# Turning the encoder's memory tokens in 32x32 blocks on VectorE, with a DMA exchange, in place of TensorE transposes

## The chip, the core and the metric

The kernel runs on one core of one Trainium2 chip. The metric is the device time of one execution in microseconds (us); the median of three runs of the kernel before is 964.87 us (964.23 to 965.66).

The core has five engines with instruction queues of their own, and each queue runs in order: PE (TensorE, matrix products), DVE (VectorE), ACT (ScalarE), POOL (GpSimd) and SP (SyncE, which here issues nearly all DMAs). An engine waits for another by semaphores. So an instruction that waits holds up everything that stands behind it on its engine.

## What is computed

Two layers over 256 tokens of width 1024. Cut to what matters here:

```
mem_n = rms_norm(mem, mem_norm)                     # 256 memory tokens x 1024
for l in range(2):
    x = x + 0.5 * rms_norm(swiglu(rms_norm(x, ng[0]), w_gu[l, 0], w_down[l, 0]), ng[1])
    h = rms_norm(x, ng[2])
    tok, qm = retention_mixer(h, ...) if l == 0 else mla_mixer(h, ...)
    mem_out = memory_attention(qm, mem_n, mem_w_kv[l])   # keys and values: mem_n @ w_kv
    x = x + rms_norm(concat([tok, mem_out]) @ w_o[l], ng[3])
    x = x + 0.5 * rms_norm(swiglu(rms_norm(x, ng[4]), w_gu[l, 1], w_down[l, 1]), ng[5])
```

`swiglu(h) = (silu(g) * u) @ w_down` with `g, u = split(h @ w_gu)` and an inner width of 2816. The memory does not depend on x, so its norm and its transposed form, which the products with `mem_w_kv` need, can be made at any time before the mixer of the layer. The kernel makes them anew in each layer.

## The kernel before

**Precision and products.** Every float32 operand of a large product is split into a high part (fp32r, a copy made by ACT) and a rest (a subtraction on DVE); `split` (line 74) makes the two. A product is then three matmuls (`mm3`, lines 136 to 138): high x high, high x low of the weights, low x high. A weight tile arrives from HBM in a buffer `raw` (128x1024, five of them), ACT writes `wh`, DVE writes `wl` (nine of each), and PE uses both. `split_raw` does this for a tile. All loads are issued by SP in the order that the scheduler chose.

**The swiglu stage (`ffn`).** The inner width is cut into 11 chunks of 256 columns. For a chunk c, `gu(t, c)` makes the gate and up products of token half t (24 matmuls of 512 columns), `swiglu(t, c)` makes `s` on ACT and `a` on DVE, and the chunk's activations are turned for the product with `w_down`: `turn` lets DVE transpose 32x32 blocks into `aT`, and for a pair of chunks 4 POOL copies and 12 DMAs (32 KB each, issued by SP) exchange the blocks between the partitions into `ag` (one buffer). `take(c)` splits the result into `ah` and `al`; it stands behind the instructions of a later swiglu (`behind`, which queues instructions behind given ones on their engine). The program order from chunk 3 on is `gu(0, c)`, `gu(1, c)`, then the extra work of the chunk, then `both(c - 3)`, which is the down product of the chunk three before, 24 matmuls. PE follows this order exactly; ACT, DVE, POOL and SP follow an order that the scheduler computed when the program was built.

**The memory (`Mem`).** In the first swiglu of each layer extra work is hooked in at chunks 6, 7 and 8 (`mem_extra`): `load(mt)` loads the 128 memory tokens of half mt (two tiles `m`, 256 KB each) and the gain (512 KB, into a `raw` buffer), computes the norm (ACT squares, DVE `ms`, POOL `rstd`, DVE scales `m`); `put(mt)` lets PE transpose the eight 128x128 blocks into two banks, from where ACT and DVE split them into `zh` and `zl`. In layer 0 the extra work of chunks 3 and 4 makes the rotary tables: `posi`, `invb` and `lgb` are loaded, DVE computes `ang`, `kk`, `rr`, ACT the sine `tab`, DVE the rest of `tab`.

The names that the text uses: `raw`, `wh`, `wl` (weights), `s`, `a`, `aT`, `ag`, `ah`, `al` (activations of the swiglu), `m`, `ms`, `rstd` (memory and its norm), `zh`, `zl` (its transposed parts), `ang`, `kk`, `rr`, `tab` (rotary tables), `gpost`, `gpre`, `lgb`, `invb` (gains and small inputs).

Of the kernel before, what the change touches and what calls it, by code (L numbers as in the profile page):

```python
# [18 lines left out]
P = 128  # L19
DM = 1024  # L20
# [11 lines left out]
def kernel(ctx, tc, x, mem, positions, norm_gains, ffn_w_gu, ffn_w_down, w_o,  # L32
# [30 lines left out]
    def raw_tile():  # L63
        return wp.tile([P, 1024], F32, name="raw", tag="raw", bufs=5)
# [31 lines left out]
        return tc.issue_after(last_load[0])  # L96

    ahead = []

    def behind(*inss):  # L100

# [102 lines left out]
    def post(t, accs, gain, half, next_gain, hook=None):  # L204
# [19 lines left out]
                hook()  # L224
        return None if next_gain is None else pre(t, next_gain)


    def gu_src(wgu, c, u):
        return (wgu[2 * u * P:(2 * u + 2) * P, :]
# [2 lines left out]
    def ffn(l, j, zs, gains, extra=(), first=None):  # L232
        wgu, wd = ffn_w_gu[l, j], ffn_w_down[l, j]
        gu_w, d_w, act, at, pair = {}, {}, {}, {}, {}
        accs = [[None, None], [None, None]]
        extra = dict(extra)
        C = NFC - 1

        def load_gu(c):
            gu_w[c] = [weights(gu_src(wgu, c, u), 1024) for u in range(KB // 2)]  # L240

        def load_d(c):
            d_w[c] = [weights(wd[c * FC + b * P:c * FC + (b + 1) * P, :], 1024) for b in range(2)]

        def gu(t, c, part=None):
            z = zs[t]
            if c not in gu_w:
                load_gu(c)
            if part != 1:
                act[t, c] = bank()  # L250
            p = act[t, c]
            for k in range(KB) if part is None else range(part * 4, part * 4 + 4):
                wh, wl = gu_w[c][k // 2]
                n = slice((k % 2) * 512, (k % 2 + 1) * 512)
                m = slice(k * P, (k + 1) * P)
                mm3(p, z.h[:, m], z.l[:, m], wh[:, n], wl[:, n], k == 0, k == KB - 1)
            if part is None:
                swiglu(t, c)

        def swiglu(t, c):  # L260
            p, z = act[t, c], zs[t]
            s = k1("s")
            s_ins = S.activation(out=s, in_=p[:, 0:FC], func=AF.Silu, scale=z.r).ins  # L263
            a = k1("a")
            a_ins = V.scalar_tensor_tensor(out=a, in0=p[:, FC:2 * FC], scalar=z.r, in1=s,  # L265
                                           op0=ALU.mult, op1=ALU.mult).ins
            if (t, c) == (1, NFC - 1) or first and (t, c) == (0, 0):
                ahead[:] = [s_ins, a_ins]
            act[t, c] = a
            if c < C:  # L270
                turn(t, c)
            for k in [k for k in list(pair) if landed(k) == (t, c)]:
                with behind(s_ins, a_ins):
                    take(k)

        def turn(t, c):


            if t == 0 and c % 2 == 0:
                pair[c] = wk.tile([P, 1024], F32, name="aT", tag="aT", bufs=2)  # L280
            b = pair[c - c % 2]
            V.transpose(out=b.rearrange("p (q u t b x) -> p u t q b x", q=4, u=2, t=2, b=2)[:, c % 2, t],  # L282
                        in_=act.pop((t, c)).rearrange("p (b q x) -> p q b x", b=2, q=4))
            if t == 1 and c % 2:
                g = wk.tile([P, 1024], F32, name="ag", tag="ag", bufs=1)
                for i in range(4):
                    sl = slice(i * 32, (i + 1) * 32)
                    G.tensor_copy(out=g[sl, i * 256:(i + 1) * 256], in_=b[sl, i * 256:(i + 1) * 256])  # L288
                    for q in range(4):
                        if q != i:  # L290
                            nc.sync.dma_start(out=g[q * 32:(q + 1) * 32, i * 256:(i + 1) * 256],  # L291
                                              in_=b[sl, q * 256:(q + 1) * 256])
                pair[c - 1], pair[c] = g, g

        def landed(c):

            return (0, min(c + 3, C)) if c % 2 == 0 else (0, C) if c + 2 > C - 1 else (1, c + 2)

        def take(c):
            g = pair.pop(c)  # L300
            ah, al = t2("ah", 512, F32R), t2("al", 512, F32R)
            for t in range(2):
                sl = slice(t * FC, (t + 1) * FC)
                split(g.rearrange("p (i u t b x) -> p u t b i x", i=4, u=2, t=2, b=2)[:, c % 2, t],
                      ah[:, sl].rearrange("p (b i x) -> p b i x", i=4, b=2),
                      al[:, sl].rearrange("p (b i x) -> p b i x", i=4, b=2))
                at[t, c] = ah[:, sl], al[:, sl]

        def tr(t, c):
            a = act.pop((t, c))  # L310
            ah, al = k1("ah", FC, F32R), k1("al", FC, F32R)
            transposed([a[:, 0:P], a[:, P:2 * P]], ah, al)
            at[t, c] = ah, al

        def down(t, c, hs=(0, 1)):
            if c not in d_w:
                load_d(c)
            ah, al = at[t, c]
            for i in hs:
                if c == 0:  # L320
                    accs[t][i] = bank()
                for b in range(2):
                    wh, wl = d_w[c][b]
                    n = slice(i * 512, (i + 1) * 512)
                    m = slice(b * P, (b + 1) * P)
                    mm3(accs[t][i], ah[:, m], al[:, m], wh[:, n], wl[:, n],
                        c == 0 and b == 0, c == NFC - 1 and b == 1)

        def both(c):
            down(0, c)  # L330
            down(1, c)

        if first:
            gu_w[0] = first
            gu(0, 0, 0)
            zs[1].put()
            gu(0, 0, 1)
            swiglu(0, 0)
            gu(1, 0)
            gu(0, 1)  # L340
        else:
            gu(0, 0)
            gu(0, 1, 0)
            zs[1].put()
            gu(0, 1, 1)
            swiglu(0, 1)
            gu(1, 0)
        gu(1, 1)
        gu(0, 2)
        gu(1, 2)  # L350
        for c in range(3, C):
            gu(0, c)
            gu(1, c)
            if c == 4:
                with behind_weights():
                    gain_post, next_gain = gains()
            if c in extra:
                with behind_weights():
                    extra[c]()
            both(c - 3)  # L360
        gu(0, C)
        both(C - 3)
        tr(0, C)
        gu(1, C, 0)
        down(0, C - 2)
        down(0, C - 1)
        down(0, C)
        gu(1, C, 1)
        with in_order():
            z0 = post(0, accs[0], gain_post, True, next_gain, lambda: swiglu(1, C))  # L370
        down(1, C - 2)
        tr(1, C)
        down(1, C - 1)
        down(1, C, (0,))
        if z0:
            z0.put()
        down(1, C, (1,))
        z1 = post(1, accs[1], gain_post, True, next_gain)
        return [z0, z1]
# [36 lines left out]
    class Mem:  # L416
# [2 lines left out]
        def __init__(self, l):  # L419
            self.l = l  # L420

        def load(self, mt):
            if mt == 0:
                self.gain = raw_tile()
                bcast(self.gain, mem_norm)
                self.T = [ztile(), ztile()]
            parts = []
            for i in range(2):
                m_ = t2("m")
                nc.sync.dma_start(out=m_, in_=mem[0, mt * P:(mt + 1) * P, i * 512:(i + 1) * 512])  # L430
                parts.append(m_)
            r = rstd_of(parts, 1.0 / 32.0, EPS, "rstd")
            for i in range(2):
                V.scalar_tensor_tensor(out=parts[i], in0=parts[i], scalar=r, in1=halves(self.gain)[i],
                                       op0=ALU.mult, op1=ALU.mult)
            self.parts = parts

        def put(self, mt):
            for i in range(2):
                tp = transposes([self.parts[i][:, j * P:(j + 1) * P] for j in range(4)])  # L440
                sub = lambda a: a.rearrange("p (j m) -> p j m", j=4)[:, :, mt * P:(mt + 1) * P]
                split(tp.rearrange("p (j m) -> p j m", j=4), sub(self.T[i][0]), sub(self.T[i][1]))

        def keys(self):
            w = k_blocks(mem_w_kv[self.l], 0, 256)
# [642 lines left out]
        V.tensor_scalar(out=nlgb, in0=lgb[:, RH:2 * RH], scalar1=-1.0, scalar2=None, op0=ALU.mult)  # L1088

    def mem_extra(m):  # L1090
        def first():
            m.load(0)

        def second():
            m.put(0)
            m.load(1)

        def third():
            m.put(1)
        return {6: first, 7: second, 8: third}  # L1100

    m0 = Mem(0)
    zs = ffn(0, 0, zs, lambda: (gpost(0, 1), gpre(0, 2)), {3: tables, 4: tables2, **mem_extra(m0)}, first=first)
    zs = retention(zs, m0, lambda: (gpost(0, 3), gpre(0, 4)))
    zs = ffn(0, 1, zs, lambda: (gpost(0, 5), gpre(1, 0)))
    m1 = Mem(1)
# [37 lines left out]
```

## Time and profile before

| | |
|---|---|
| median of 3 runs | 964.87 us |
| the profiled execution | 965.5 us |
| its span (first to last instruction) | 963.7 us |
| PE busy | 949.9 us (99%) |
| DVE busy | 626.2 us (65%) |
| ACT busy | 516.2 us (54%) |
| POOL busy | 87.5 us (9%) |
| DMA queue of SP | 148608 packets, 188.38 MB, 61.2% |
| granted TensorE clock | 0.999 |

The profiled execution lies 1.8 us above its own span and 0.6 us above the median. A matmul's duration in the profile overlaps the next one's, since matmuls are pipelined; what a matmul costs is the distance between the starts of two that follow each other.

### The profile page before, as it was taken

How to read it: one execution, taken by the hardware profiler on the slowest of the kernel's cores; microseconds unless marked ns; L12 is line 12 of the kernel's file. 1: busy time of each engine (PE TensorE's matmuls, PEld its weight loads, DVE VectorE, ACT ScalarE, POOL GpSimd, SP SyncE). 2: the span in 40 equal slices, each digit the busy share in tenths (PEclk: the TensorE clock that was granted, in tenths of full speed). 3: DMA queues.
4: the chain of work that ended last, by engine and by line, in shares of the span. 5: the costliest groups of instructions: out<-in, count | busy, mean ns of one | idle time of the engine just before them, and what ended most of it. 6: DMA issues, size and time to landing. Idle time of an engine off the chain costs nothing.

```text
span 963.7 us, 13202 instructions
## 1 busy us (share of the span) xinstructions
PE 949.9 (99%) x4503; PEld 789.2 (82%) x4503; DVE 626.2 (65%) x989; ACT 516.2 (54%) x859; POOL 87.5 (9%) x122
## 2 busy tenths in 40 slices
PE   8999999999999999999999999999999999999997
PEld 6887888898878888888887888888897888888886
DVE  6766567586886775655558656655666886566552
ACT  6535456465665654544446444555568864444441
POOL 0110111010000111101101111101010011111010
PEclk9999999999999999999999999999999999999999
DMA  8668677493645556867546676875561746777631
GB/s 276 213 221 274 208 226 249 133 313 103 208 156 162 153 149 234 288 209 211 173 127 204 217 243 223 260 240 165 155 204 32 231 125 198 238 238 225 221 104 44
DMA packets 148679, 189.23 MB, mean 196 GB/s; under 512 B 13314, under 2 KB 130818, under 8 KB 148611
## 3 DMA queue, kind: packets, MB, share of 16 engines
q1 hardware_dynamic: 148608, 188.38, 61.2%
q8 instruction: 35, 0.57, 0.2%
q14 instruction: 34, 0.27, 0.1%
q10 hardware_dynamic: 2, 0.00, 0.0%
HBM read 179.42 MB, written 1.05 MB: 187 GB/s over the span
## 4 chain that ended last, share of the span: by engine, by line
PE 81%; DMA 7%; DVE 4%; ACT 3%; issue 3%; SPq 2%; POOL 0%; DVEq 0%; POOLq 0%; ACTq 0%
PE bank L138 26%; PE bank L136 26%; PE bank L137 26%; DMA raw<-in_ffn_w_gu_dram 4%; PE bank L162 2%; DVE wl L76 2%; ACT wh L75 2%; SPq L291 1%; DMA raw<-in_ret_w_in_dram 1%; DMA raw<-in_ffn_w_down_dram 1%; PE bank L493 1%; SPq L87 1%; ACT e L504 0%; DMA gpre<-in_norm_gains_dram 0%; DVE x L220 0%
## 5 line engine op out<-in xcount | busy, mean ns | idle before, releaser
L76 DVE TENSOR_TENSOR wl<-raw,wh 128x1024 fp32r<-128x1024 f32 (+2 forms) x326 | 388.6, 1209 | 164.6 <-ACT wh L75 158.2
L75 ACT CAST wh<-raw 128x1024 fp32r<-128x1024 f32 (+2 forms) x326 | 334.7, 1042 | 216.5 <-PE bank L138 78.4
L136 PE MATMUL bank<-wh,zh 128*128 128x512 f32 (+2 forms) x944 | 364.5, 386 | 0.6 <-ACT zh L75 0.4
L137 PE MATMUL bank<-wl,zh 128*128 128x512 f32 (+2 forms) x944 | 360.4, 382 | 0.6 <-DVE wl L76 0.6
L138 PE MATMUL bank<-wh,zl 128*128 128x512 f32 (+2 forms) x944 | 360.5, 382 | 0.4 <-DVE zl L76 0.4
L138 PEld LDWEIGHTS bank<-wh,zl 128*128 128x128 f32 x944 | 177.4, 188 | 35.4 <-DVE zl L76 1.4
L136 PEld LDWEIGHTS bank<-wh,zh 128*128 128x128 f32 x944 | 177.6, 188 | 34.8 <-ACT zh L75 0.9
L137 PEld LDWEIGHTS bank<-wl,zh 128*128 128x128 f32 x944 | 177.6, 188 | 34.5 <-DVE wl L76 1.6
L136 PE MATMUL bank<-wh,ah 128*128 128x512 f32 x352 | 138.0, 392 | 0.0
L138 PE MATMUL bank<-wh,al 128*128 128x512 f32 x352 | 137.4, 390 | 0.6 <-DVE al L76 0.6
L137 PE MATMUL bank<-wl,ah 128*128 128x512 f32 x352 | 137.0, 389 | 0.0
L288 POOL COPY ag<-aT 32x256 f32<-32x256 f32 x80 | 55.9, 699 | 481.6 <-DMA raw<-in_ffn_w_gu_dram 290.2
L263 ACT ACTIVATE s<-bank,rstd 128x256 f32<-128x256 f32 x88 | 41.5, 472 | 101.0 <-PE bank L138 100.9
L265 DVE SCALAR_TENSOR_TENSOR a<-bank,rstd,s 128x256 f32<-128x256 f32 x88 | 42.3, 480 | 59.5 <-ACT s L263 59.3
L138 PEld LDWEIGHTS bank<-wh,al 128*128 128x128 f32 x352 | 66.1, 188 | 15.2 <-DVE al L76 1.5
L137 PEld LDWEIGHTS bank<-wl,ah 128*128 128x128 f32 x352 | 66.1, 188 | 13.4
L136 PEld LDWEIGHTS bank<-wh,ah 128*128 128x128 f32 x352 | 66.1, 188 | 13.4 <-ACT ah L75 0.2
L147 ACT ACTIVATE junk<-bank 128x512 bf16<-128x512 f32 x24 | 14.3, 594 | 41.8 <-DVE y L209 29.4
L282 DVE STREAM_TRANSPOSE aT<-a 128x256 f32<-128x256 f32 x80 | 35.4, 443 | 1.5
L75 ACT CAST zh<-bank 128x512 fp32r<-128x512 f32 (+2 forms) x58 | 25.3, 462 | 19.4 <-PE bank L162 12.4
L76 DVE TENSOR_TENSOR zl<-bank,zh 128x512 fp32r<-128x512 f32 (+2 forms) x58 | 28.7, 519 | 6.0 <-ACT zh L75 6.0
L76 DVE TENSOR_TENSOR al<-ag,ah 128x256 fp32r<-128x256 f32 x80 | 31.3, 404 | 1.0 <-ACT ah L75 0.8
(154 smaller groups left out, 519.6 us busy)
## 6 DMA issues: line engine op xcount, KB each, us to landing
raw<-in_ffn_w_gu_dram SPq DMA_DIRECT2D x352, 256.0 KB, 4.7
raw<-in_ffn_w_down_dram SPq DMA_DIRECT2D x88, 512.0 KB, 5.4
raw<-in_ret_w_in_dram SPq DMA_DIRECT2D x48, 256.0 KB, 4.7
raw<-in_w_o_dram SPq DMA_DIRECT2D x16, 512.0 KB, 4.3
ag<-aT SPq DMA_DIRECT2D x240, 32.0 KB, 1.9
raw<-in_mem_w_kv_dram SPq DMA_DIRECT2D x8, 512.0 KB, 5.4
gpost<-in_norm_gains_dram SPq DMA_DIRECT2D x6, 512.0 KB, 6.2
gpre<-in_norm_gains_dram SPq DMA_DIRECT2D x5, 512.0 KB, 7.6
```

The lines of the kernel that those rows point to most:

```text
L75: ins = S.copy(out=hi, in_=src).ins
L76: V.tensor_tensor(out=lo, in0=src, in1=hi.bitcast(F32), op=ALU.subtract)
L87: last_load[0] = nc.sync.dma_start(out=dst[:, k], in_=src[:, k]).ins
L136: T.matmul(out=dst, lhsT=ah, rhs=bh, start=start, stop=False)
L137: T.matmul(out=dst, lhsT=ah, rhs=bl, start=False, stop=False)
L138: T.matmul(out=dst, lhsT=al, rhs=bh, start=False, stop=stop)
L147: S.activation(out=junk[:, :h.shape[1]], in_=h, func=AF.Square, scale=scale, accum_out=ss[:, i:i + 1])
L162: T.transpose(out=tp[:s.shape[1], j * P:(j + 1) * P], in_=s, identity=ident)
L263: s_ins = S.activation(out=s, in_=p[:, 0:FC], func=AF.Silu, scale=z.r).ins
L265: a_ins = V.scalar_tensor_tensor(out=a, in0=p[:, FC:2 * FC], scalar=z.r, in1=s, op0=ALU.mult, op1=ALU.mult).ins
L282: V.transpose(out=b.rearrange("p (q u t b x) -> p u t q b x", q=4, u=2, t=2, b=2)[:, c % 2, t], in_=act.pop((t, c)).rearrange("p (b q x) - ...
L288: G.tensor_copy(out=g[sl, i * 256:(i + 1) * 256], in_=b[sl, i * 256:(i + 1) * 256])
```

## The change

The four memory tiles and the gain are loaded together at chunk 3; the gain now lies in a buffer of the tag `A` (two buffers), not in a `raw`. The norms are made at chunks 4 and 5, each queued behind the swiglu just before (`latest`). At chunk 6 `turn(0)` lets DVE transpose one half of the columns of both token halves in 32x32 blocks into `mT`, and `exchange` (which is the code that stood in the swiglu's `turn`) makes 4 POOL copies and 12 DMAs into `mg`. At chunk 8 `take(0)` splits it and `turn(1)` does the other half of the columns; chunk 9 takes that. PE's 32 transposes of the memory are gone. The rotary tables keep their chunks 3 and 4, after the memory's part of the same chunk.

```diff
+    def exchange(b, g):
+        for i in range(4):
+            sl = slice(i * 32, (i + 1) * 32)
+            G.tensor_copy(out=g[sl, i * 256:(i + 1) * 256], in_=b[sl, i * 256:(i + 1) * 256])
+            for q in range(4):
+                if q != i:
+                    nc.sync.dma_start(out=g[q * 32:(q + 1) * 32, i * 256:(i + 1) * 256],
+                                      in_=b[sl, q * 256:(q + 1) * 256])
...
+            latest[:] = [s_ins, a_ins]
...
-        def load(self, mt):
-            if mt == 0:
-                self.gain = raw_tile()
...
-        def put(self, mt):
-            for i in range(2):
-                tp = transposes([self.parts[i][:, j * P:(j + 1) * P] for j in range(4)])
...
+        def load(self):
+            self.gain = wk.tile([P, DM], F32, name="mgain", tag="A", bufs=2)
+            bcast(self.gain, mem_norm)
+            self.T = [ztile(), ztile()]
+            self.parts = [[t2("m") for i in range(2)] for mt in range(2)]
+            for mt in range(2):
+                for i in range(2):
+                    nc.sync.dma_start(out=self.parts[mt][i], in_=mem[0, mt * P:(mt + 1) * P, i * 512:(i + 1) * 512])
+        def norm(self, mt):
+            parts = self.parts[mt]
+            with behind(*latest):
+                r = rstd_of(parts, 1.0 / 32.0, EPS, "rstd")
...
+        def turn(self, i):
+            b = wk.tile([P, 1024], F32, name="mT", tag="A", bufs=2)
+            with behind(*latest):
+                for mt in range(2):
+                    V.transpose(out=b.rearrange("p (q u j x) -> p u q j x", q=4, u=2, j=4)[:, mt],
+                                in_=self.parts[mt][i].rearrange("p (j q x) -> p q j x", j=4, q=4))
+            self.g = wk.tile([P, 1024], F32, name="mg", tag="A", bufs=2)
+            exchange(b, self.g)
...
+        def take(self, i):
+            th, tl = self.T[i]
+            with behind(*latest):
+                for mt in range(2):
...
+                    split(self.g.rearrange("p (i u j x) -> p u j i x", i=4, u=2, j=4)[:, mt], sub(th), sub(tl))
...
-        return {6: first, 7: second, 8: third}
+        def eighth():
+            m.take(0)
+            m.turn(1)
+        return {3: m.load, 4: lambda: m.norm(0), 5: lambda: m.norm(1), 6: lambda: m.turn(0), 8: eighth,
+                9: lambda: m.take(1)}
```

The order that the scheduler made of it changes in more places than these. First SP in the first swiglu of layer 0, from the gate and up loads of chunks 0 to 3 to those of chunk 6 (two rows of 256 KB make one `raw` tile; the 12 rows `ag<-aT` are one exchange). Before:

```order
L87 DMA raw<-in_ffn_w_gu_dram 128x2x256 x2
L291 DMA ag<-aT 32x256 x12
L87 DMA raw<-in_ffn_w_gu_dram 128x2x256 x6
L67 DMA gpost<-in_norm_gains_dram 128x1024
L67 DMA gpre<-in_norm_gains_dram 128x1024
L67 DMA lgb<-in_ret_log_decay_dram 128x12
L89 DMA raw<-in_ffn_w_down_dram 128x1024 x2
L87 DMA raw<-in_ffn_w_gu_dram 128x2x256 x3
L597 DMA invb<-in_inv_freq_dram 128x80
L87 DMA raw<-in_ffn_w_gu_dram 128x2x256 x2
L291 DMA ag<-aT 32x256 x12
L87 DMA raw<-in_ffn_w_gu_dram 128x2x256 x3
```

And now, on the same engine from the same exchange:

```order
L235 DMA ag<-aT 32x256 x12
L87 DMA raw<-in_ffn_w_gu_dram 128x2x256 x8
L67 DMA gpost<-in_norm_gains_dram 128x1024
L67 DMA gpre<-in_norm_gains_dram 128x1024
L67 DMA lgb<-in_ret_log_decay_dram 128x12
L89 DMA raw<-in_ffn_w_down_dram 128x1024 x2
L87 DMA raw<-in_ffn_w_gu_dram 128x2x256
L435 DMA m<-in_mem_dram 128x512 x2
L235 DMA ag<-aT 32x256 x12
L435 DMA m<-in_mem_dram 128x512 x2
L614 DMA invb<-in_inv_freq_dram 128x80
L87 DMA raw<-in_ffn_w_gu_dram 128x2x256 x7
```

Chunk 4's first tile moved behind the first exchange; of chunk 5's eight half tiles one stands before the second exchange and seven behind it, two memory tiles and `invb`, where five stood before it and three behind.

Next DVE in the same stage, from the second half of chunk 4's work to the first `al` of chunk 2. Before:

```order
L76 TENSOR_TENSOR wl<-raw,wh 128x1024 x3
L265 SCALAR_TENSOR_TENSOR a<-bank,rstd,s 128x256
L282 STREAM_TRANSPOSE aT<-a 128x4x64
L76 TENSOR_TENSOR wl<-raw,wh 128x1024 x4
L265 SCALAR_TENSOR_TENSOR a<-bank,rstd,s 128x256
L76 TENSOR_TENSOR al<-ag,ah 128x256
```

And now, from the last `kk` through chunk 5's four weight tiles into the `rr` that stand ahead of that `al`:

```order
L627 TENSOR_SCALAR kk<-kk 128x320
L76 TENSOR_TENSOR wl<-raw,wh 128x1024 x2
L276 SCALAR_TENSOR_TENSOR a<-bank,rstd,s 128x256
L294 STREAM_TRANSPOSE aT<-a 128x4x64
L76 TENSOR_TENSOR wl<-raw,wh 128x1024
L152 SCALAR_TENSOR_TENSOR ms<-ss 128x1
L442 SCALAR_TENSOR_TENSOR m<-m,rstd,mgain 128x512 x2
L76 TENSOR_TENSOR wl<-raw,wh 128x1024
L630 SCALAR_TENSOR_TENSOR rr<-kk,ang 128x160 x2
L76 TENSOR_TENSOR wl<-raw,wh 128x1024
L632 SCALAR_TENSOR_TENSOR rr<-kk,rr 128x320
```

The first part of the tables (`ang`, `kk`) now stands ahead of all four `wl` of chunk 5, the norm of the first memory half ahead of the fourth of them, and the rest of the tables (`rr`, `tab`) between there and the `al`; before, all of it stood ahead of the rows shown.

Last DVE in the first swiglu of layer 1, from the fourth `wl` of chunk 5 to the first `al` of chunk 2. Before:

```order
L76 TENSOR_TENSOR wl<-raw,wh 128x1024 x3
L265 SCALAR_TENSOR_TENSOR a<-bank,rstd,s 128x256
L76 TENSOR_TENSOR al<-ag,ah 128x256
L282 STREAM_TRANSPOSE aT<-a 128x4x64
L76 TENSOR_TENSOR al<-ag,ah 128x256
```

And now:

```order
L76 TENSOR_TENSOR wl<-raw,wh 128x1024
L276 SCALAR_TENSOR_TENSOR a<-bank,rstd,s 128x256
L294 STREAM_TRANSPOSE aT<-a 128x4x64
L76 TENSOR_TENSOR wl<-raw,wh 128x1024
L152 SCALAR_TENSOR_TENSOR ms<-ss 128x1
L442 SCALAR_TENSOR_TENSOR m<-m,rstd,mgain 128x512 x2
L76 TENSOR_TENSOR wl<-raw,wh 128x1024 x4
L276 SCALAR_TENSOR_TENSOR a<-bank,rstd,s 128x256
L76 TENSOR_TENSOR al<-ag,ah 128x256
L294 STREAM_TRANSPOSE aT<-a 128x4x64
L76 TENSOR_TENSOR al<-ag,ah 128x256
```

The norm of the first memory half moved from behind this `al` to a place ahead of it, with four `wl` in between.

## Rows read from the trace of the kernel before

**Rows 1.** The page: PE, its granted clock by slices, two groups of DVE.

```profile
PE 949.9 (99%) x4503; PEld 789.2 (82%) x4503; DVE 626.2 (65%) x989; ACT 516.2 (54%) x859; POOL 87.5 (9%) x122
...
PEclk9999999999999999999999999999999999999999
...
L265 DVE SCALAR_TENSOR_TENSOR a<-bank,rstd,s 128x256 f32<-128x256 f32 x88 | 42.3, 480 | 59.5 <-ACT s L263 59.3
...
L282 DVE STREAM_TRANSPOSE aT<-a 128x256 f32<-128x256 f32 x80 | 35.4, 443 | 1.5
```

**Rows 2.** Timeline of PE: start, us, engine, line, operation, tiles, shape, count [idle before].

```profile
121.95 0.40 PE L138 MATMUL bank<-wh,zl 128*128 128x512 f32 x1
122.18 1.04 PE L162 MATMUL bank<-ident,m 128*128 128x128 f32 x8
122.98 0.47 PE L136 MATMUL bank<-wh,ah 128*128 128x512 f32 x1
123.29 0.40 PE L137 MATMUL bank<-wl,ah 128*128 128x512 f32 x1
```

**Rows 3.** The memory's tile `m`, all its transposes: count, ns min/median/max.

```profile
L162 PE MATMUL bank<-ident,m x32: 270/272/276, 122.2 to 638.3; 128*128 128x128 f32 x32
```

**Rows 4.** Timeline of PE, first swiglu of layer 0: three matmuls.

```profile
56.26 0.50 PE L138 MATMUL bank<-wh,al 128*128 128x512 f32 x1
...
77.93 0.39 PE L137 MATMUL bank<-wl,zh 128*128 128x512 f32 x1
...
89.83 0.50 PE L138 MATMUL bank<-wh,al 128*128 128x512 f32 x1 [0.60 <-DVE al L76]
```

**Rows 5.** Timeline of DVE, 54 to 60 us.

```profile
54.25 1.22 DVE L76 TENSOR_TENSOR wl<-raw,wh 128x1024 fp32r<-128x1024 f32 x1 [1.97 <-ACT wh L75]
...
55.79 0.41 DVE L76 TENSOR_TENSOR al<-ag,ah 128x256 fp32r<-128x256 f32 x1
...
59.37 0.17 DVE L1088 TENSOR_SCALAR nlgb<-lgb 128x6 f32<-128x6 f32 x1 [1.37 <-DMA lgb<-in_ret_log_decay_dram]
```

**Rows 6.** Timeline of SP's queue, 45 to 73 us: loads, exchange, loads.

```profile
46.08 4.22 SPq L87 DMA_DIRECT2D raw<-in_ffn_w_gu_dram  x6
...
64.32 7.55 SPq L291 DMA_DIRECT2D ag<-aT  x12
71.92 1.26 SPq L87 DMA_DIRECT2D raw<-in_ffn_w_gu_dram  x2
```

**Rows 7.** Line 87's loads after an exchange: the two at 71.9 us, third and fourth at 47.5.

```profile
DMA to landing us min/median/max: 3.3/3.3/3.3
...
DMA to landing us min/median/max: 5.0/5.0/5.0
```

**Rows 8.** Timeline of DVE, 65 to 73 us: ends of the two parts of the rotary tables.

```profile
65.31 0.57 DVE L604 TENSOR_SCALAR ang<-invb,posf 128x80 f32<-128x80 f32 x2
...
68.20 0.33 DVE L610 TENSOR_SCALAR kk<-kk 128x320 f32<-128x320 f32 x1
...
69.58 0.55 DVE L613 SCALAR_TENSOR_TENSOR rr<-kk,ang 128x160 f32<-128x160 f32 x2
...
72.84 0.17 DVE L629 TENSOR_SCALAR tab<-tab 128x16 f32<-128x16 f32 x1
```

**Rows 9.** Timeline of DVE, 84 to 104 us: weights, the `al` of chunk 2, a norm.

```profile
84.35 4.71 DVE L76 TENSOR_TENSOR wl<-raw,wh 128x1024 fp32r<-128x1024 f32 x4
...
89.36 0.41 DVE L76 TENSOR_TENSOR al<-ag,ah 128x256 fp32r<-128x256 f32 x1
...
103.43 1.42 DVE L434 SCALAR_TENSOR_TENSOR m<-m,rstd,raw 128x512 f32<-128x512 f32 x2 [0.73 <-POOL rstd L141]
```

**Rows 10.** Timelines of SP, PE and DVE, first swiglu of layer 1.

```profile
561.31 8.42 SPq L291 DMA_DIRECT2D ag<-aT  x12
...
588.09 0.39 PE L138 MATMUL bank<-wh,al 128*128 128x512 f32 x1
...
583.30 0.42 DVE L76 TENSOR_TENSOR al<-ag,ah 128x256 fp32r<-128x256 f32 x1
```

More of the change, by code (lines that the diff above doesn't have):

```diff
@@ L98 @@
     ahead = []
+    latest = []
     def behind(*inss):
@@ L285, in turn @@
                 g = wk.tile([P, 1024], F32, name="ag", tag="ag", bufs=1)
[L286 to L292, printed above, removed]
+                exchange(b, g)
                 pair[c - 1], pair[c] = g, g
@@ L420, in __init__ @@
             self.l = l
-        def load(self, mt):
-            if mt == 0:
-                self.gain = raw_tile()
-                bcast(self.gain, mem_norm)
-                self.T = [ztile(), ztile()]
-            parts = []
-            for i in range(2):
[L429 to L436, printed above, removed]
@@ L438, in put @@
-        def put(self, mt):
-            for i in range(2):
-                tp = transposes([self.parts[i][:, j * P:(j + 1) * P] for j in range(4)])
-                sub = lambda a: a.rearrange("p (j m) -> p j m", j=4)[:, :, mt * P:(mt + 1) * P]
-                split(tp.rearrange("p (j m) -> p j m", j=4), sub(self.T[i][0]), sub(self.T[i][1]))
+        def load(self):
[6 more added lines that the diff above has]
+                    nc.sync.dma_start(out=self.parts[mt][i], in_=mem[0, mt * P:(mt + 1) * P, i * 512:(i + 1) * 512])
@@ new lines, in norm @@
+        def norm(self, mt):
+            parts = self.parts[mt]
+            with behind(*latest):
+                r = rstd_of(parts, 1.0 / 32.0, EPS, "rstd")
+                for i in range(2):
+                    V.scalar_tensor_tensor(out=parts[i], in0=parts[i], scalar=r, in1=halves(self.gain)[i],
+                                           op0=ALU.mult, op1=ALU.mult)
+        def turn(self, i):
[6 more added lines that the diff above has]
+            exchange(b, self.g)
@@ L444, in keys @@
+        def take(self, i):
+            th, tl = self.T[i]
+            with behind(*latest):
+                for mt in range(2):
+                    sub = lambda a: a.rearrange("p (j u i x) -> p u j i x", j=4, u=2, i=4)[:, mt]
+                    split(self.g.rearrange("p (i u j x) -> p u j i x", i=4, u=2, j=4)[:, mt], sub(th), sub(tl))
         def keys(self):
@@ L1090, in mem_extra @@
     def mem_extra(m):
[L1091 to L1099, printed above, removed]
-        return {6: first, 7: second, 8: third}
+        def eighth():
[3 more added lines that the diff above has]
+                9: lambda: m.take(1)}
     m0 = Mem(0)
-    zs = ffn(0, 0, zs, lambda: (gpost(0, 1), gpre(0, 2)), {3: tables, 4: tables2, **mem_extra(m0)}, first=first)
+    e0 = mem_extra(m0)
+    zs = ffn(0, 0, zs, lambda: (gpost(0, 1), gpre(0, 2)), {**e0, 3: lambda: (e0[3](), tables()), 4: lambda: (e0[4](), tables2())}, first=first)
     zs = retention(zs, m0, lambda: (gpost(0, 3), gpre(0, 4)))
```

## The prediction

> **What bounds the kernel now.** I read the page first: PE is busy 99% of the span, in every slice at a granted clock of nine tenths or more, which is the upper of its two levels (2.4 GHz) [rows 1]. DVE has a third of its time free and ACT nearly half. So a matmul that goes is worth its distance to the next, and nothing else in the kernel is worth anything unless PE waits for it. The timeline of PE says what that distance is: a matmul of 512 columns starts 0.23 us after the one before (121.95 to 122.18) [rows 2]. Then I looked for the places where PE comes close to waiting, because the change moves work on the queues behind it. In the first swiglu of layer 0 there are two, both at the third matmul of a down product, the first that needs `al`. At 56.26 PE starts as soon as the `al` of DVE at 55.79 has ended (55.79 + 0.41 = 56.20) [rows 4, 5]. At 89.83 it has waited 0.60 for the `al` at 89.36 [rows 4, 9]. There DVE has no slack at all: the `al` stands in its queue behind `wl` of weights, these behind `wh` of ACT, these behind loads, and the loads behind an exchange on SP. In layer 1 the same `al` ends at 583.72 and is used at 588.09: 4.4 us of slack [rows 10].
>
> **What goes.** The 32 transposes run in four groups of eight. Eight start at 122.18, the next matmul at 122.98, and the one after 0.31 later instead of 0.23 [rows 2]: 0.80 + 0.08 = 0.88 us per group, 3.5 us in all. All four groups lie behind the places treated below, so the gain is not eaten by them.
>
> The Trainium skill ("TensorE: Matmul & The Clock Gate", Part 4: PE-mode transpose) gives about 275 ns for a transpose in a kernel, and the trace has the same duration, 270 to 276 ns [rows 3]. But durations overlap: by starts one costs 0.11 us here. By the skill's figure the saving would be 32 x 0.275 = 8.8 us, an estimate from that page; by the starts it is 3.5, and the sum goes by these.
>
> **What comes, and is hidden.** Four DVE transposes of 512 columns per layer: 443 ns for 256 columns [rows 1], so between 0.44 and 0.89 each; I take 0.89, 3.5 us a layer, in chunks 6 and 8. Four exchanges of 12 issues, 7.6 to 8.4 us of SP each [rows 6, 10], with 16 POOL copies. The splits of the memory read `mg` instead of a bank, with the same count; I take no difference. By chunk 6 PE is late already (below), which gives the weights as much more slack; a swiglu chunk lasts 16 us of PE (72 matmuls), an exchange blocks SP for half of that, and its result is not needed before the mixer. The cost is nothing if it holds; if that cover were gone, the block of an exchange, 7.6 us, less the slack of the loads behind it (which I put at 4 at the least) would be 3 to 4 us per place. The gain tile no longer occupies a `raw`: worth nothing where PE does not wait for loads.
>
> **What is moved to where PE has no slack.** Three steps in layer 0.
>
> First, chunk 4's first tile now stands behind the first exchange, so DVE and ACT handle the third tile after it, not the second, ahead of the first `al`. Six loads took SP 4.22 us [rows 6], so two more make 1.4 us. DVE's `wl` at 54.25 [rows 5], which waits for the load, becomes one at 55.7, `al` ends at 57.6 and PE starts at 57.7 instead of 56.26: **1.4 us late**. Bounds: 0.6 (one load) and 2.0.
>
> Second, chunk 5. The `nlgb` that stands ahead of the next `al` waits for `lgb`, at 59.37 [rows 5]; two loads more ahead of it make 60.8. Then `a`, `al`, `aT`, `al`, about 1.5 us by their durations less overlaps, free the one `ag` buffer at 62.3 and SP starts the exchange, two us earlier than the 64.32 of before. It ends 7.55 us later [rows 6], at 69.9. Now come two memory tiles, 0.6 us each, and `invb`, issued at 71.1. The first two loads after an exchange land after 3.3 us, the third and fourth after 5.0 [rows 7]; `invb` is the third and lands at 76.1. DVE's `ang` and `kk` wait for it: 65.31 to 68.53 with one `wl` of 1.18 inside is 2.0 us [rows 8, 9], so 78.1. Two `wl` of 1.18 (4.71 for four [rows 9]): 80.5. `a` and `aT`, 0.48 + 0.44 [rows 1]: 81.4. Third `wl`: 82.6. The norm, the wait for `rstd` 0.73 and the scaling 1.42 [rows 9], with `ms` and the gaps between them about 2.3: 84.9. Fourth `wl`: 86.1. PE used its first `wl` of this chunk at 77.93 [rows 4], the fourth 18 matmuls later, at 82.0. So PE is **4.1 us late**, the 1.4 included. The loads of the last two tiles, issued up to 75.5, land by 81 and are not late themselves.
>
> Third, the `al` of chunk 2. Behind that `wl` DVE has the rest of the tables (69.58 to 73.01, the wait for ACT's `tab` included: 3.4 us [rows 8]), four `wl` (4.7), `a` and `aT` (0.9) and the `al` (0.41): 9.4 us, so it ends at 95.5, and PE's matmul of 89.83 starts then: **5.7 us late in all**. This includes the 0.6 that PE already waited there. Bounds for the three together: 3.7, if the loads behind the exchange land 2 us earlier (3.3 and not 5.0), and 7.7, if the wait for a slot or a lane adds as much as the 1 us by which layer 1's exchange exceeds this one, twice.
>
> Layer 1 has no tables. Its first exchange also has one tile more behind it, 1.3 us, so the second begins at about 562.6 where it began at 561.31 [rows 10], and takes 8 us: 570.6. Three memory tiles and then chunk 5's last tile are queued there; its second half is issued at 573.0 and lands 5.0 later, 578.0. `wh` and `wl`: 580.2. Then `a`, `aT` 0.9, `wl` 1.2, norm 2.3, four `wl` 4.7, `a` and `al` 0.9: 590.2. PE wants it at 588.09 [rows 10]: **2.0 us late**, between 0 and 3.5.
>
> **Sum.** 5.7 + 2.0 - 3.5 = +4.2 us. The profiled execution took 965.5 (span 963.7 and 1.8 around it); by it the new time is 969.7, and against the median of 964.87 it is **969.1**. Lower bound 3.7 + 0 - 3.5 = +0.2, upper 7.7 + 3.5 - 3.5 = +7.7.
>
> **Rivals.** *The waits fit in.* If loads behind an exchange land after 3.3 us throughout and DVE works while it waits now, layer 0 loses 3.7, layer 1 nothing: 965.1, no change. For it: the first two loads do land so, and DVE is idle a third of the time. Against: in before the third and fourth do not [rows 7], and DVE's queue is in order, so its idle time ahead of `ang` can't be used.
>
> *The gain stands alone.* PE loses only the first 1.4 us or nothing: 962.8 to 961.4. It needs chunk 5's first tile and `invb` to be there 4 us earlier, that is, a second exchange that starts at 58 and not 62. For it: nothing but the slack of 7 to 10 us that these tiles have in other chunks; against: the order puts seven of eight halves behind it.
>
> *A transpose costs PE its duration.* Then 8.7 us go (32 x 272 ns [rows 3]), and with the same waits 964.87 + 7.7 - 8.7 = 963.9. Against: the starts in [rows 2].
>
> *The exchanges delay weights too.* SP is held a further 7.6 us in chunks 6 and 8 of each layer. If the `al` of chunk 4 or the weights of chunk 9 come late by 3 us at one place in each layer, 975. It decides when a wait in SP's queue lasts beyond the 4 us of slack that I put above. Against it: PE's own lateness.
>
> **Chances.** Forecast 0.52, exchanges that delay weights too 0.10, waits fit in 0.17, gain alone 0.17, transposes at their duration 0.04. A change under 0.2% (1.9 us) can't be told from none. So slower 0.62, the same 0.17, faster 0.21. The forecast's own range is 966.8 to 972.6; with the rivals until two in ten are left out, 962.0 to 973.5.
>
> **What would show it.** PE's busy time down by some us, no `ident,m` rows; PE's waits in the first 100 us up from about 2 to about 7: at the third matmul of the first down product (57.7), at the last two weight tiles of chunk 5 (around 84), at the `al` of chunk 2 (95), and in layer 1 at the same `al`. SP's exchange at 62.3 and `invb` landing at 76. From 100 us on PE runs without waits to the mixer; the `mg` exchanges wait for nobody on PE. I am wrong if `invb` lands before 73, or if the `al` of layer 1 is there by 588, or if PE waits in chunks 7 to 10.

## The result and the profile after

The changed kernel takes 970.48 us (median of 12 runs, 966.3 to 973.98), the kernel before beside it 964.71: a ratio of 1.0062 (95% interval 1.0049 to 1.0074), slower by 5.8 us. The forecast was 969.1 and slower. The runs now scatter over 7.7 us, those of before over 3.9 (963.44 to 967.29, 12 runs).

The profiled execution took 972.66 us, its span is 970.9, so it lies 2.2 above the median and 7.2 above the span of before. From the page of the changed kernel, PE and its granted clock by slices, to be set beside [rows 1]:

```profile
PE 950.1 (98%) x4471; PEld 786.2 (81%) x4471; DVE 632.1 (65%) x997; ACT 515.5 (53%) x859; POOL 111.0 (11%) x138
...
PEclk9999999999999999999999999999999999999999
```

PE has 32 instructions fewer, as many as there were transposes, and is busy for as long as before. That can't be read as "the transposes were free": a stretch at a lower clock (below) makes busy time longer, and in the one kernel of the experiments that has none of the new waits (POOL, tables in `e`, norms at chunks 5 and 6) PE is busy 946.2 us, 3.7 less than before. The waits are in the span, not here. So the next view is what PE waited for, first in the kernel before, then in the changed one (us in total, times, longest):

```profile
PE bank L525 <- ACT pT L516: 1.4, 2, 0.9
...
PE bank L138 <- DVE al L76: 0.6, 1, 0.6
PE bank L137 <- DVE wl L76: 0.6, 2, 0.3
```

```profile
PE bank L139 <- DVE al L76: 4.0, 4, 2.0
PE bank L137 <- ACT ah L75: 2.7, 3, 1.5
...
PE bank L138 <- DVE wl L76: 2.2, 3, 1.7
...
PE bank L542 <- ACT pT L533: 0.4, 1, 0.4
```

`al`, `ah` and `wl` together made 1.2 us of waiting (PE's product lines moved by one) and now make 8.9. The timeline of PE says where (start, us, ..., [idle before]); each row is compared with the same matmul of before:

```profile
57.09 0.50 PE L137 MATMUL bank<-wh,ah 128*128 128x512 f32 x1 [1.51 <-ACT ah L75]
...
58.41 0.50 PE L139 MATMUL bank<-wh,al 128*128 128x512 f32 x1 [0.58 <-DVE al L76]
...
86.41 0.50 PE L138 MATMUL bank<-wl,zh 128*128 128x512 f32 x1 [1.69 <-DVE wl L76]
...
94.56 0.50 PE L139 MATMUL bank<-wh,al 128*128 128x512 f32 x1 [0.82 <-DVE al L76]
...
126.92 0.39 PE L137 MATMUL bank<-wh,ah 128*128 128x512 f32 x1
...
180.14 0.50 PE L137 MATMUL bank<-wh,ah 128*128 128x512 f32 x1 [0.68 <-ACT ah L75]
...
558.42 0.39 PE L138 MATMUL bank<-wl,ah 128*128 128x512 f32 x1
559.36 0.50 PE L139 MATMUL bank<-wh,al 128*128 128x512 f32 x1 [0.55 <-DVE al L76]
...
592.54 0.50 PE L137 MATMUL bank<-wh,ah 128*128 128x512 f32 x1 [0.55 <-ACT ah L75]
...
595.29 0.50 PE L139 MATMUL bank<-wh,al 128*128 128x512 f32 x1 [2.01 <-DVE al L76]
```

And three rows of PE in the kernel before that these are held against:

```profile
175.90 0.39 PE L136 MATMUL bank<-wh,ah 128*128 128x512 f32 x1
...
555.22 0.39 PE L137 MATMUL bank<-wl,ah 128*128 128x512 f32 x1
555.45 0.39 PE L138 MATMUL bank<-wh,al 128*128 128x512 f32 x1
```

Read as lateness: 58.41 - 56.26 [rows 4] = 2.15; at 86.41 it is 4.4, the fourth weight tile having been used at 82.0 before; 94.56 - 89.83 [rows 4] = 4.73; 126.92 - 122.98 [rows 2] = 3.94, one group of transposes less; 180.14 - 175.90 = 4.24 after two groups, so 1.2 was lost between; 558.42 - 555.22 = 3.20 at the start of layer 1 (the mixer gave back 1.0: the wait for `pT` shrank); 559.36 - 555.45 = 3.91; 595.29 - 588.09 [rows 10] = 7.20. All of this is one execution, and not the median one. Behind the last wait comes the last surprise, which windows show (stretch, length, busy us of PE, PEld, DVE, ACT, POOL, granted clock, DMA share, GB/s):

```profile
590.00:596.00 6.00, 3.44 (x14) 2.23 (x13) 6.00 (x9) 4.60 (x7) 0.00 (x0) 1.00 0.78 261
596.00:600.00 4.00, 4.00 (x13) 3.11 (x12) 4.00 (x6) 3.27 (x7) 0.00 (x0) 0.57 0.96 322
600.00:604.00 4.00, 4.00 (x19) 3.31 (x18) 2.09 (x5) 2.94 (x5) 3.04 (x5) 1.00 0.91 265
```

In 4 us PE starts 13 matmuls and then 19: after two waits, 0.55 for `ah` and 2.01 for `al`, the granted clock is near its lower level (1.2 GHz) for some 3.5 us, with starts 0.43 apart and not 0.23. Eight matmuls at 0.20 more each, 1.6 us, 1.8 with its edges. Layer 1's two groups of transposes take 1.8 off again, and the end is 7.2 late.

What SP and DVE did in layer 0. SP's queue of the changed kernel:

```profile
39.22 7.76 SPq L235 DMA_DIRECT2D ag<-aT  x12
47.08 5.59 SPq L87 DMA_DIRECT2D raw<-in_ffn_w_gu_dram  x8
...
63.51 7.54 SPq L235 DMA_DIRECT2D ag<-aT  x12
71.15 1.00 SPq L435 DMA_DIRECT2D m<-in_mem_dram  x2
72.20 0.42 SPq L614 DMA_DIRECT2D invb<-in_inv_freq_dram  x1
...
155.49 7.54 SPq L235 DMA_DIRECT2D mg<-mT  x12
163.13 6.24 SPq L89 DMA_DIRECT2D raw<-in_ffn_w_down_dram  x6
170.46 7.83 SPq L235 DMA_DIRECT2D ag<-aT  x12
```

DVE from there to the `al` of chunk 2, and the same place in layer 1:

```profile
76.60 0.43 DVE L621 TENSOR_SCALAR ang<-invb,posf 128x80 f32<-128x80 f32 x2 [5.99 <-DMA invb<-in_inv_freq_dram]
...
83.81 1.41 DVE L442 SCALAR_TENSOR_TENSOR m<-m,rstd,mgain 128x512 f32<-128x512 f32 x2 [0.73 <-POOL rstd L142]
85.14 1.22 DVE L76 TENSOR_TENSOR wl<-raw,wh 128x1024 fp32r<-128x1024 f32 x1
86.28 0.55 DVE L630 SCALAR_TENSOR_TENSOR rr<-kk,ang 128x160 f32<-128x160 f32 x2
...
94.12 0.71 DVE L76 TENSOR_TENSOR al<-ag,ah 128x256 fp32r<-128x256 f32 x2
...
588.55 1.42 DVE L442 SCALAR_TENSOR_TENSOR m<-m,rstd,mgain 128x512 f32<-128x512 f32 x2 [0.73 <-POOL rstd L142]
589.88 4.63 DVE L76 TENSOR_TENSOR wl<-raw,wh 128x1024 fp32r<-128x1024 f32 x4
...
594.82 0.42 DVE L76 TENSOR_TENSOR al<-ag,ah 128x256 fp32r<-128x256 f32 x1
```

So the losses are where the memory's loads and norms met chunks 4 and 5, plus a stretch of lower clock. Four causes can be behind that: the place of the memory's DMAs in SP's queue, the norms in DVE's queue, the exchanges, and (seen only in the experiments) a pool of buffers.

### The profile page after: what moved, and what is told of

Read it like the earlier page. It is cut to its first block, busy times and chain, and to the rows that moved or that the text cites. A ratio compares the mean times of both kernels' runs of the same rounds, so it can differ in the third digit from the quotient of the medians.

```text
span 970.9 us, 13230 instructions
## 1 busy us (share of the span) xinstructions
PE 950.1 (98%) x4471; PEld 786.2 (81%) x4471; DVE 632.1 (65%) x997; ACT 515.5 (53%) x859; POOL 111.0 (11%) x138
## 4 chain that ended last, share of the span: by engine, by line
PE 69%; DMA 9%; SPq 8%; DVE 6%; issue 4%; ACT 3%; POOL 0%; DVEq 0%; POOLq 0%; ACTq 0%
PE bank L139 22%; PE bank L137 22%; PE bank L138 22%; SPq L235 5%; DMA raw<-in_ffn_w_gu_dram 4%; DMA raw<-in_ffn_w_down_dram 3%; DVE wl L76 3%; PE bank L163 2%; ACT wh L75 2%; SPq L87 1%; DMA lgb<-in_ret_log_decay_dram 1%; PE bank L510 1%; PE bank L762 1%; PE bank L748 1%; DVE a L276 1%
## 5 line engine op out<-in xcount | busy, mean ns | idle before, releaser
L232 POOL COPY ag<-aT 32x256 f32<-32x256 f32 x80 | 62.0, 775 | 397.9 <-DMA raw<-in_ffn_w_gu_dram 202.7
L75 ACT CAST ah<-ag 128x256 fp32r<-128x256 f32 x80 | 27.8, 401 | 9.5 <-DMA ag<-aT 9.2
L75 ACT CAST zh<-bank 128x512 fp32r<-128x512 f32 (+2 forms) x50 | 21.0, 443 | 19.5 <-PE bank L163 12.5
```

The costliest lines, as they stand in the source:

```text
L75: ins = S.copy(out=hi, in_=src).ins
```

## The experiments

**Everything later.** Load at chunk 5, both norms and the first turn at chunk 6.

```diff
-        return {3: m.load, 4: lambda: m.norm(0), 5: lambda: m.norm(1), 6: lambda: m.turn(0), 8: eighth,
-                9: lambda: m.take(1)}
+        return {5: m.load, 6: sixth, 8: eighth, 9: lambda: m.take(1)}
...
```

Here `sixth` calls `norm(0)`, `norm(1)` and `turn(0)`.

> Load of the memory at chunk 5 instead of 3, both norms and the first turn at chunk 6, the rest as in the changed kernel. Theory (the cost is what the early load and the early norms put ahead of the weights of chunks 4 and 5): the waits of the changed kernel at 57, 83 to 86 and 94 us and those of layer 1 at 559 and 592 to 595 go, the 3.5 us of the transposes remain as a gain, and the wait of 1.3 us at 176 to 180 may stay: 961.2 to 962.5 us. Rival (the four exchanges and the added DVE transposes cost what was lost): 970, as the changed kernel. Rival (the transposes were covered by something else on PE): 964.7, as before.

970.62 us, ratio 1.0062 (1.0043 to 1.0081): as slow as the changed kernel. Missed by 8 us, and instructive: from 20 to 95 us the waits for weights and activations shrank from 4.6 to 2.0 us, but others came. Timelines of DVE and PE in this kernel:

```profile
159.79 0.41 DVE L76 TENSOR_TENSOR al<-ag,ah 128x256 fp32r<-128x256 f32 x1
...
157.28 0.39 PE L138 MATMUL bank<-wl,ah 128*128 128x512 f32 x1
160.25 0.50 PE L139 MATMUL bank<-wh,al 128*128 128x512 f32 x1 [2.59 <-DVE al L76]
```

And the same `al` in the changed kernel:

```profile
159.44 0.41 DVE L76 TENSOR_TENSOR al<-ag,ah 128x256 fp32r<-128x256 f32 x1
...
160.01 0.39 PE L139 MATMUL bank<-wh,al 128*128 128x512 f32 x1
```

The wait for this `al` is longer than any of the changed kernel, the lower clock follows it too (granted 0.57 from 161 to 165 us, matmuls 0.42 apart), and layer 1 waits at 655 to 679. In the changed kernel the `al` comes at nearly the same time, but PE is 3 us late there and uses it 0.16 us after its end: its lateness hides the place. Here PE is 0.4 us late, and the wait shows.

What sets that `al` can be read in the changed kernel: ACT's `wh` at 148.65 has waited 8.23 us for a down weight. SP issued the first load of these weights at 143.55, behind two exchanges that began at 119.23 (the memory's) and 135.95; before it was 138.16, behind one. That speaks for the rival that named the exchanges, which also had the time right. With the exchange issued by POOL (below) the same `al` is there at 154.77. That the exchange alone makes this wait is argued: no run takes it out of this kernel, and with the norms at chunks 5 and 6 (the last kernel below) the `al` came at 156.97 behind the same exchanges, without a wait.

**Only the norms later.** Loads as in the changed kernel, norms at chunk 6.

```diff
+        return {3: m.load, 6: sixth, 8: eighth, 9: lambda: m.take(1)}
...
```

> Loads at chunk 3 as in the changed kernel, but both norms at chunk 6 with the first turn. SP's order of the first 80 us is the changed kernel's, only the norms leave DVE and ACT there. Theory (loads and norms each have a share): the waits at 57 us (2.2) and about 83 (0.4) stay, the one at 86 (2.0) goes with the 2.2 us of norm ahead of that weight tile, in layer 1 the wait for al at 595 (2.3) goes and with it the stretch at half clock behind it (1.6), the wait for ah there (0.8) stays: about 964.5 us. Rival (loads alone): 970. Rival (norms alone): 961 to 962.

971.11 us, 1.0073 (1.0054 to 1.0092): 6.6 above the theory, by the time the rival of the loads alone. The waits at 86 and for the `al` at 595 shrank as expected (lateness at the second 2.9 and not 7.2) and the one at 57 stayed. But here the clock fell behind that one (granted 0.57 from 58 to 62 us), 1.5 us were lost at 178 and 3.1 at 655 to 678. As in the run before, waits that went early came back later. That both norms at chunk 6 do it, by delaying the turn and its exchange in SP's queue, is argued, not shown.

**No exchange of the memory.**

```diff
-            self.g = wk.tile([P, 1024], F32, name="mg", tag="A", bufs=2)
-            exchange(b, self.g)
+            self.g = b
```

> The exchange of the memory (16 POOL copies and 48 DMAs in all) is left out: take reads the turned tile itself, so the memory's blocks are not in their places; all else is as in the changed kernel. Theory (exchanges are hidden but for one place): only the 1.3 us at 176 to 180 us, where an exchange stands ahead of a down weight, go: 969 us. Rival (the exchanges are the cost, through SP and the DMA queues): 961 to 964 us.

968.36 us, 1.0043 (1.0031 to 1.0056): 1.8 us less than the changed kernel by the ratios, near the theory's 969. The wait at 176 to 180 is gone. DVE's order differs in other places too, so only that wait is read from this kernel; the time excludes the exchanges as the main cost.

**No norm in layer 1.** The scaling, `ms` and `rstd` are made for `self.l == 0` alone.

> In layer 1 alone the norm of the memory is left out (no squares, ms, rstd and scaling; the products use the memory as loaded); layer 0 as in the changed kernel. Theory (the al of chunk 2 in layer 1 is late by the norm, and the fall of the clock comes from that wait): the wait of 2.3 us goes, the clock stays at its upper level, together 3.9 us: 966.6. Rival (the clock falls there for another reason): 968.2. Rival (the loads behind the exchange set that al): 970.5, no change.

967.46 us, 1.0032 (1.0021 to 1.0044): 2.9 less, between the theory's 3.9 and the rival's 2.3, and the interval holds both. PE starts the matmul with `al` at 589.83 without a wait, and the clock stays:

```profile
590.00:594.00 4.00, 4.00 (x18) 3.31 (x19) 3.02 (x5) 3.32 (x4) 0.00 (x0) 1.00 0.95 337
```

So the norm is the price of that `al`, and without the wait the clock does not fall here. A wait of this length does not always bring the fall, though: in the kernel without the exchange PE waits 2.10 us for this `al` (592.97), in the next one 2.14 (594.46), and the granted clock stays at 1.00 behind both. That the median gains less than 3.9 fits a fall that not every execution has: the 12 runs of the changed kernel granted mean clocks of 0.993 to 1.000, the lowest with 973.98 us, the highest with 967.06.

**The exchange issued by POOL.**

```diff
-                    nc.sync.dma_start(out=g[q * 32:(q + 1) * 32, i * 256:(i + 1) * 256],
+                    (eng or nc.sync).dma_start(out=g[q * 32:(q + 1) * 32, i * 256:(i + 1) * 256],
...
+            exchange(b, self.g, nc.gpsimd)
```

> The changed kernel with the 12 DMAs of each memory exchange issued by POOL, behind its own copies, in place of SP; loads and norms stay. Theory (an exchange costs by what stands behind it in SP's queue): the wait of 1.3 us at 176 to 180 us goes, those of the chunks before 6 stay: about 969 us, like the kernel without the exchange (968.4). Rival (an exchange costs by its traffic on the DMA queues, whoever issues it): 970.5, unchanged. Rival (POOL issues slowly and the ag copies behind it come late): 972 or more, with new waits for ah after 118 and 155 us.

970.93 us, 1.0061 (1.0041 to 1.0080): near the first rival's 970.5, but the interval holds the theory's 969 too. By the trace the wait at 176 to 180 is gone as the theory said, and 1.6 us of waits for `wh` and `wl` at 583.7 to 585 are new. POOL's issuing need not be their cause: the kernel with the tables in `e` and the exchanges on SP (below) has 1.3 us of them at the same place. The cause was not isolated; the early waits are still there.

**Gain and memory loads by POOL as well,** behind the `ag` copies of chunk 3 on POOL.

```diff
+            with behind(last_copy[0]):
+                nc.gpsimd.dma_start(out=self.gain, in_=mem_norm.partition_broadcast(P))
...
+                        nc.gpsimd.dma_start(out=self.parts[mt][i],
```

> As the one with POOL's exchange, and the gain and the four memory tiles are issued by POOL too, behind the copies of the exchange of chunks 2 and 3 (63 us). So SP's order is that of the kernel before with the memory's rows taken out; the norms stay in DVE's order at the end of chunks 4 and 5. Theory (SP's order makes the waits at 57 and 83 us and in layer 1 those at 559 and the ah at 592; DVE's norms make those at 86 and 595): the first go, the second shrink, since weights arrive 2 to 3 us earlier and the wl behind the norm with them: 961.5 to 964 us. Rival (DVE's norms and transposes are enough by themselves): 966 to 968, with the waits for wl at 86 and for al at 595 left. Rival (DMAs of POOL take bandwidth or start so late that the norm waits for m): 970 and a wait of DVE for m.

968.07 us, 1.0038 (1.0026 to 1.0051): outside the theory's 961.5 to 964. From 20 to 88 us only 0.44 us of wait is left, for the `al` at 56.43; the waits for the `al` at 559 and for the `ah` at 592 are gone, and the `al` behind it is waited for 0.74 us (592.49) and not 2.01. One wait is new, larger than any before. PE, then ACT:

```profile
94.21 0.80 PE L138 MATMUL bank<-wh,ah 128*128 128x512 f32 x1 [5.26 <-ACT ah L75]
```

```profile
92.76 0.75 ACT L647 ACTIVATE tab<-rr 128x128 f32<-128x128 f32 x4 [4.24 <-DVE rr L638]
...
93.77 0.70 ACT L75 CAST ah<-ag 128x256 fp32r<-128x256 f32 x2
```

`ah` stands in ACT's queue behind `tab`, `tab` waits for `rr`, and `rr` starts at 88.5 although `kk` was there at 70.6 (in the kernel before `rr` starts at 69.58 [rows 8]). `rr` is a tile of `t2`, eight buffers, of which four are now held by `m` from chunk 3 on.

**The tables out of `t2`,** in the kernel with POOL and, apart, in the changed kernel.

```diff
-        ang, kk, rr = t2("ang", 2 * NI), t2("kk", 4 * NI), t2("rr", 4 * NI)
+        ang, kk, rr = (esm(n)[:, :w * NI] for n, w in (("ang", 2), ("kk", 4), ("rr", 4)))
```

> The kernel with all of the memory's DMAs on POOL, and the rotary tables' ang, kk and rr in buffers of the tag e (free in this stage) and not of t2. In that kernel the only large wait left was the one for ah at 88.6 us (5.4, and 1.6 to 2.0 of half clock behind it); rr stood at 88.45 and tab behind it. Theory (four m tiles hold half of t2's eight buffers from chunk 3 on, so rr waits for a buffer that PE frees late, and the ah behind it too): rr goes to 70 us, the wait and the half clock go, 968.1 - 5.4 - 1.8 = 961 us. Rival (the wait for ah was the norm's place in DVE's order): 966 to 968, the wait stays within 2 us of what it was. Rival (another wait takes its place at the fourth weight tile of chunk 5): 963 to 966.

962.31 us, 0.9976 (0.9967 to 0.9986): faster than before, 1.3 above the theory. `rr` starts at 69.8 and the wait for `ah` is gone. The timeline of PE in the profiled execution (965.08, the slowest of the 11) shows what is left, with a granted clock of 0.61 behind it (92 to 96 us):

```profile
90.90 0.50 PE L140 MATMUL bank<-wh,al 128*128 128x512 f32 x1 [1.94 <-DVE al L76]
```

In the changed kernel with the same edit alone:

> The changed kernel with only that: ang, kk and rr in buffers of the tag e, SP's order of the first 80 us as in the changed kernel. Theory (there the first thing that is late is invb, behind the second exchange; t2 only decides where rr stands): the al of chunk 2 (0.2 us) is on time, but rr and tab now stand ahead of the last two weight tiles of chunk 5, whose waits grow by up to 2 us: 970 to 972.5. Rival (t2's buffers are the cause in the changed kernel too): 964 to 967.

968.69 us, 1.0045 (1.0030 to 1.0060): below the theory's 970 to 972.5, above the rival's 964 to 967. The trace shows the step: PE no longer waits for the `al` of chunk 2, but for the third and the fourth weight tile of chunk 5, 0.64 and 2.12 us, where it was 1.69 for the fourth. The lateness at 94.78 is 5.0 us, near the 4.7 of the changed kernel, but made of other parts: the first step is only 0.7 in this execution, and the clock fell behind the 2.12 (granted 0.57 from 87 to 91 us). `t2` alone is not the cause. What the edit does to the kernel before was not run; there `rr` starts at 69.58, 1 us behind the last `kk` [rows 8].

**The norms behind the `al` of chunk 2,** one at chunk 5, one at chunk 6, in the kernel with POOL and the tables in `e`.

```diff
+        return {3: m.load, 5: lambda: m.norm(0), 6: sixth, 8: eighth, 9: lambda: m.take(1)}
...
```

Here `sixth` calls `norm(1)` and `turn(0)`.

> The kernel with the memory's DMAs on POOL and the tables in e, and the norms one chunk later (chunk 5, and chunk 6 ahead of the second half of the first turn). In DVE's order the al of chunk 2 then has no norm ahead of it. Theory (the waits left there, 1.9 us for the al at 90 in layer 0 with 1.6 of half clock behind it in the profiled execution, and 1.1 at 588 in layer 1, are the norm's 2.3 us): both go, and in those executions that fell to half clock that too: 962.3 - 2.5 to 3 = 959 to 960 us. Rival (with the norm at chunk 6 the turn is late and the al of chunks 8 and 9 with it, as when both norms stood there): 963 to 966, with waits for al or ah at 155 to 180 and 655 to 680.

961.15 us (960.0 to 961.72), 0.9960 (0.9946 to 0.9974), 3.4 us below the kernel before, above the theory's 959 to 960 and below the rival's 963. The interval overlaps that of the version before, so what moving the norms gave is read from the waits for `al` (2.9 us there), not from the time. What PE waits for in it:

```profile
PE bank L140 <- DVE al L76: 0.6, 1, 0.6
PE bank L139 <- DVE wl L76: 0.6, 2, 0.3
```

That is the 1.2 of the kernel before for these tiles, and the times scatter over 1.7 us. The transposes' 3.5 us are all there. PE in this kernel, at the down product behind each layer's second group of transposes:

```profile
154.68 0.39 PE L138 MATMUL bank<-wh,ah 128*128 128x512 f32 x1
...
649.74 0.39 PE L138 MATMUL bank<-wh,ah 128*128 128x512 f32 x1
```

Before, these two started at 156.61 and 654.70, so they are 1.9 and 5.0 us early. At the down products ahead of each layer's first group (105.72 and 600.78, before 105.86 and 603.96) it was 0.1 and 3.2. The groups gave 1.8 us in each layer, 3.6 in all.

**The same with all DMAs on SP again.**

> The version with the norms at chunks 5 and 6 and the tables in e, but with all of the memory's DMAs on SP again, as in the changed kernel. Theory (the place in SP's queue is a cause of its own): the waits at 56 to 58 us, at the first and the last weight tiles of chunk 5 (80 to 87), and one for ah at 175 to 180 come back, layer 1 keeps a part of its own at 555 to 595, without the norm's 2.3: 965.5 to 968. Rival (the norms' place and t2's buffers are the whole cause, the queue does not matter): 961, as with POOL.

966.64 us, 1.0020 (1.0007 to 1.0032), inside the theory's range: the memory's DMAs cost 5.5 us more on SP than on POOL (5.8 by the ratios). Its waits, on the same view:

```profile
PE bank L138 <- DVE wl L76: 2.1, 5, 0.8
PE bank L137 <- ACT ah L75: 2.0, 2, 1.0
PE bank L139 <- DVE al L76: 1.8, 4, 0.6
```

The Trainium skill ("Trainium Kernel Development and Optimization", Key Constraints) says that DMAs issued by SP, ACT and POOL share the same 16 DMA engines, so that issuing from several engines saves the issue time only. These two kernels agree: on POOL the DMAs of the memory's exchange land after 3.4 us (median; 1.9 on SP), and still the kernel is 5.5 us faster, since what it cost was SP's time.

## Why the prediction came out as it did

The side was right and the time within 1.4 us of the median. The mechanism was right in kind, its terms were not all of the right size, and one was missing; that the sum came so near is partly luck.

- *What goes, 3.5 us:* right. Matmuls that a group stood between now follow each other without them (lateness 4.73 at 94.56, 3.94 at 126.92), and in the kernel without the waits the four groups gave 3.6. The rival of 8.7 us has fallen. (The groups do not all lie behind the places treated, as the prediction says: layer 0's two lie ahead of layer 1's place. The sum does not change by it.)
- *First step, 1.4 us (0.6 to 2.0):* 2.15 in this execution, outside its bounds. The two loads were right, but the next load behind the exchange was issued a microsecond later (47.08, not 46.08 [rows 6]), which the sum did not have, and PE waited first for `ah`. That microsecond need not be the change's: the six kernels of the experiments that have the same DMAs on SP up to there began the exchange at 38.2 to 39.2 (39.22 here), and were 0.7, 1.5, 1.7, 1.8, 1.8 and 3.0 us late at this matmul. So the term was near, a little small, and single executions scatter around it.
- *Second step, 4.1 late:* 4.4. Every link was near: exchange 63.5 (62.3), `invb` at 76.6 (76.1), norm done at 85.2 (84.9), fourth `wl` at 86.4 (86.1).
- *Third step, 5.7 late:* 4.7. DVE was done 1.0 earlier (94.5, not 95.5), because `rr` stood among the `wl`, so that no wait for ACT was left open. Why `rr` stood there at all, the `t2` buffers held by `m`, was not in the prediction; with the loads off SP it alone made a 5.26 us wait.
- *Layer 1, 2.0 us (0 to 3.5):* 4.0 by starts (7.20 - 3.20), 0.5 outside its bounds, and 3.9 to 5.0 in the three kernels that keep these loads and norms (without the exchange, POOL's exchange, tables in `e`). This term was too small. The same shift at the first exchange that was counted in layer 0 (0.7 at 559) was not counted here as a wait of PE, the second exchange began at 567.19, 1.4 later than 562.6 and PE's lateness of 3.2 give, and `ah` was late too. Leaving out the norm shows its part.
- *The clock:* missing. The prediction had every wait cost what it lasts. In the profiled execution one wait cost 1.6 more; in the executions of the other kernels it was now this wait, now another, now none.
- *Exchanges at no cost:* nearly. The rival had 3 us at one place in each layer; it is 1.2 at one place in layer 0. An exchange stood ahead of a down weight (163.13, after 155.49), DVE's `al` behind that weight freed `ag` late, and the next `ag` exchange began at 170.46. The two experiments without it on SP show it gone. So PE did wait in the last down products (0.68 at 180.14), which the prediction named as a sign of being wrong. The reason that it gave, PE's lateness as cover for the exchanges, held at 160 us with 0.16 us to spare; in the kernel with everything later the cover was gone, and PE waited there.
- *PE's busy time down by some us:* not seen in the changed kernel (950.1), but in the kernel without the waits (946.2).
- *Not foreseen in the other direction:* 1.0 us in the mixer, where a wait for `pT` went.

In sum, from the differences of starts: 2.15 + 2.25 + 0.33 - 1.76 + 1.2 - 1.0 + 4.0 + 1.76 - 1.76 = 7.2. The median lies 2.2 below that execution. So the sum came out near partly by luck: the missing clock and the size of layer 1 were offset by the third step, the mixer, and executions that lost less.

Shown: that SP's queue, the norm ahead of the `al`, and `t2`'s buffers each decide waits, and that without all three the gain of the transposes stands. Only argued: which share each has in the changed kernel by itself, since removing one lets the scheduler move others.

## What to carry to other kernels

Work taken off the bounding engine pays only if the work that replaces it has a queue with room. Ask of every new instruction not what it takes but what is queued behind it on each in-order engine, DMA issues included, and which pool's buffers it holds for how long. If a step is moved and the waits move with it, change the queue instead.

## What the runs showed of the hardware

- After waits of PE of about 2 us the granted clock could fall to its lower level: 596 to 600 us behind waits of 0.55 and 2.01 (granted 0.57), behind 2.59 at 160 in the kernel with everything later, behind 1.94 at 90.9 with POOL and `e`, behind 1.45 and 0.58 at 57 to 58 with only the norms later. Each time seven or eight matmuls started 0.42 to 0.43 apart and not 0.23, about 1.6 us. It did not fall after 1.51 and 0.58 at 57 to 58 in the changed kernel, nor after 2.14 at 594 with POOL's exchange or 2.10 at 593 without an exchange. So a wait can cost more than it lasts, not every time, and the length of the wait alone does not tell when.
- On POOL a DMA of an exchange is issued in 0.50 us, on SP in 0.59, and it lands later. From the instructions on the tile `mg` in the fastest kernel (count, ns min/median/max; in the changed kernel 572/588/596 ns and 1.8/1.9/4.1 us):

```profile
L236 POOL DMA_DIRECT2D mg<-mT x48: 496/496/544, 116.5 to 645.6; - x48
...
DMA to landing us min/median/max: 1.7/3.4/6.2
```

The later landing cost nothing that shows: POOL had room for the issues (13% busy), and SP's time was what the weights needed.
